# A two-layer hybrid trunk on one core: four quads instead of three begin with the first token half, and partial results move between PSUM banks

## The chip, the core and the metric

One core of a Trainium2 chip runs the whole program. TensorE (PE) multiplies into PSUM, eight banks of 128 x 512 float32 here; VectorE (DVE) and ScalarE (ACT) read PSUM and SBUF; GpSimd (POOL) and SyncE (SP) issue transfers, and POOL computes a few small things. Each of these engines has a queue of its own and works through it in order. The metric is device microseconds for one execution; three were timed before.

## The reference

512 tokens of 1024 features go through two layers: an mLSTM mixer with its MLP, then a short gated convolution with its MLP. All is float32.

```python
def sqrelu_mlp(x, w_up, w_down):
    h = jax.nn.relu(x @ w_up)
    return (h * h) @ w_down

def reference(...):
    for i in range(DEPTH):
        g = norm_g[i]
        h = rms_norm(x, g[0])
        if i % N_MIXERS == 0:
            h = mlstm_mixer(h, ...)
        else:
            h = short_conv_mixer(h, ...)
        x = x + rms_norm(h, g[1])
        h = sqrelu_mlp(rms_norm(x, g[2]), w_mlp_up[i], w_mlp_down[i])
        x = x + rms_norm(h, g[3])
    return x
```

The convolution mixer multiplies x by a 1024 x 3072 matrix, takes three gates from the result, runs a causal three-tap filter over tokens, and multiplies by a 1024 x 1024 matrix.

## The kernel before, in words

Float32 products run as three passes: every operand is split into a high part (ACT casts it to fp32r, line 80) and the remainder (DVE subtracts, line 81), and `mm3` (lines 115 to 117) multiplies high by high, high by low and low by high into the same bank.

The up-projections of the two MLPs and the input product of the convolution (the phases here called mlp 0, conv and mlp 1) are cut into quads. A quad is 512 columns of the weight. It cuts tokens, inner dimension and columns in two and needs seven products of quarter size in place of eight, in the manner of Strassen and Winograd; `prod` is one of the seven, 24 matmuls of 128 x 256. `Seven` makes the token-side factors: `a11` and `a12` from the first token half, and `p1`, `n2`, `r3`, `p4`, `a22` with differences that need the second half. `Quad` makes the weight-side ones: block(0,0) is a, block(0,1) b, block(1,1) d, block(1,0) c; a+b, then a+d, b+d and a+c are summed by DVE in place, and each is split.

Within a quad, x collects f1·a11 (`begin`) and f2·a12 (`first_done`), and is the quarter (0, 0) of the result. y starts as minus the value of x after its first product and takes n2 and r3; z takes p1 and p4; o starts as minus y and takes a22. s5 and s2 are copies of z and y in the middle (lines 875 and 877).

Before a phase stands `last_product` of the phase before. It makes 512 x 1024 in four token tiles of 128, each in two halves of the columns. After each tile comes its tail: mean square (ACT, line 181), the power -0.5 (POOL, line 173), the residual (DVE, line 274), the next norm (line 181, line 173, and DVE at line 252), and eight transposes on PE (line 261). The transposes are put off by `LATE` microseconds of counted matmul time. While the last tile's tail is under way, PE has the work that `enter` gives it: those products of the first `AHEAD` = 3 quads that need the first token half alone. Their bank x comes from the group `pu` (four banks); after the first product minus x is put aside into SBUF (line 843), and `run` copies it back into y (line 858). `last_product` and the down-projection use the group `pd` (two banks), transposes the group `pt` (two).

A scheduler then sets the order within each engine, so the order on the chip is not quite that of the code.

Of the kernel before, what the change touches and what calls it, by code (L numbers as in the profile page):

```python
# [32 lines left out]
LATE = 10.4  # L33
BLOCK = 5.2
PROD = 2.86
AHEAD = 3


@with_exitstack
def tile_hybrid_trunk(  # L40
# [158 lines left out]
    class Seven:  # L199
# [11 lines left out]
        def take(self, t, q, tp):  # L211
            c = slice((t % 2) * P, (t % 2 + 1) * P)
            a = tp.rearrange("p (k n) -> p k n", k=4)
            if t < 2:
                if t == 0:
                    self.keep[q] = raw_tile([4, 256])
                self.part(("a11", "a12")[q], c, a)
                nc.scalar.copy(self.keep[q][:, :, c], a)
                return
            if q == 0:  # L220
                self.first = a
                return
            tt = nc.vector.tensor_tensor
            k0, k1 = (k[:, :, c] for k in self.keep)

            def temp():
                return half_kb().rearrange("p (k n) -> p k n", k=4)

            s22, r3, p1 = temp(), temp(), temp()
            nc.scalar.copy(s22, a)  # L230
            tt(out=p1, in0=self.first, in1=s22, op=ALU.subtract)
            tt(out=r3, in0=self.first, in1=k0, op=ALU.subtract)
            self.part("p1", c, p1)
            tt(out=k0, in0=k0, in1=p1, op=ALU.subtract)
            self.part("n2", c, k0)
            self.part("r3", c, r3)
            tt(out=k1, in0=k1, in1=k0, op=ALU.subtract)
            self.part("p4", c, k1)
            self.part("a22", c, s22)

    def halves(n=2):
        return [slice(i * D // n, (i + 1) * D // n) for i in range(n)]
# [37 lines left out]
    def last_product(wm, r0, hT, g, tail, accs=None, ends=False, ahead=None):  # L280

        flush()
        ws = {}
        parts = [halves() for _ in range(NT)]
        if ends:
            parts[NT - 1] = halves()[:1] + halves(4)[2:]
        ygs = [[] for _ in range(NT)]
        mss = [None] * NT

        def ks(o, t, cs, k0, k1):  # L290
            hf, c0 = divmod(cs.start, 512)
            n = cs.stop - cs.start
            for k in range(k0, k1):
                w = ws[hf][k // 2]
                mm3(
                    o[:, 0:n],
                    rows_of(hT, k, t),
                    (w[:, 0, k % 2, c0 : c0 + n], w[:, 1, k % 2, c0 : c0 + n]),
                    k == 0,
                    k == KO - 1,  # L300
                )

        def done(o, t, cs):
            n = cs.stop - cs.start
            step(BLOCK * n / 512)
            i = len(ygs[t])
            if i == 0:
                mss[t] = small(len(parts[t]))
            yg = half_kb(n=n)
            ygs[t].append((cs, yg))  # L310
            last = i == len(parts[t]) - 1
            o = o[:, 0:n]
            if accs is None:
                part_ms(o, mss[t], i)
                nc.vector.tensor_tensor(out=yg, in0=o, in1=g[:, cs], op=ALU.mult)  # L315
            else:
                y = accs[t][:, cs]
                nc.vector.tensor_tensor(out=y, in0=y, in1=o, op=ALU.add)  # L318
                part_ms(y, mss[t], i)
                eng = nc.vector if ends and t == NT - 1 else nc.gpsimd  # L320
                eng.tensor_tensor(out=yg, in0=y, in1=g[:, cs], op=ALU.mult)
            if last:
                tail(t, ygs[t], mss[t])

        for hf in range(2):
            ws[hf] = [
                piece(
                    wm[r0 + 2 * i * P : r0 + 2 * (i + 1) * P, halves()[hf]].rearrange(
                        "(k p) m -> p k m", p=P
                    ),  # L330
                    2,
                )
                for i in range(4)
            ]
            os = [pd() for _ in range(2)]
            first = KO - 2 if hf == 0 else 0
            for t in range(2):
                ks(os[t], t, parts[t][hf], 0, first)
            for t in range(2):
                ks(os[t], t, parts[t][hf], first, KO)  # L340
                done(os[t], t, parts[t][hf])
        for t in range(2, NT):
            if ahead is not None:
                ahead()
            for cs in parts[t]:
                o = pd()
                ks(o, t, cs, 0, KO)
                done(o, t, cs)
# [457 lines left out]
    class Quad:  # L806
# [27 lines left out]
        def prepare_more(self):  # L834
            self.f2 = self.factor(self.block(1, 0))

        def begin(self):
            self.x = pu()
            prod(self.x, self.f1, self.xT.f["a11"], True)

        def set_aside(self):
            self.s1 = self.values()
            nc.scalar.mul(self.s1, by_tile(self.x), -1.0)

        def first_done(self):
            prod(self.x, self.f2, self.xT.f["a12"], False)
            self.take(0, 0, self.values(), by_tile(self.x))

        def run(self, begun):


            tt = nc.vector.tensor_tensor
            f = self.xT.f
            self.claim()
            a, b = self.block(0, 0), self.block(0, 1)
            y = pu()
            if begun:
                nc.scalar.copy(by_tile(y), self.s1)
            else:
                self.f1 = self.factor(a)  # L860
                self.begin()
                nc.scalar.mul(by_tile(y), by_tile(self.x), -1.0)
            tt(out=a, in0=a, in1=b, op=ALU.add)
            f5 = self.factor(a)
            z = pu()
            if not begun:
                prod(z, f5, f["p1"], True)
            d = self.block(1, 1)
            tt(out=a, in0=a, in1=d, op=ALU.add)
            f6 = self.factor(a)  # L870
            prod(y, f6, f["n2"], False)
            if begun:
                prod(z, f5, f["p1"], True)
            s5 = self.values()
            nc.scalar.copy(s5, by_tile(z))  # L875
            s2 = self.values()
            nc.scalar.copy(s2, by_tile(y))
            c = self.block(1, 0)
            if not begun:
                self.f2 = self.factor(c)  # L880
                self.first_done()
            tt(out=b, in0=b, in1=d, op=ALU.add)
            prod(y, self.factor(b), f["r3"], False)
            o = pu()
            nc.scalar.mul(by_tile(o), by_tile(y), -1.0)
            prod(z, self.factor(d), f["p4"], False)
            tt(out=s5, in0=by_tile(y), in1=s5, op=ALU.add)
            self.take(1, 1, s5, None)
            tt(out=s2, in0=by_tile(z), in1=s2, op=ALU.add)
            self.take(1, 0, s2, None)  # L890
            tt(out=a, in0=a, in1=c, op=ALU.add)
            prod(o, self.factor(a), f["a22"], False)
            self.take(0, 1, self.values(), by_tile(o))

    def enter(quads):


        for qd in quads:
            qd.prepare()
        yield  # L900
        for qd in quads:
            qd.prepare_more()
        yield
        flush(2)
        for qd in quads:
            qd.begin()
            qd.set_aside()
        for qd in quads:
            qd.first_done()
        flush()  # L910

    def by_tile(o):
# [65 lines left out]
    def conv(xT, gain_of, tail_of, ahead):  # L978
# [5 lines left out]
        def gated(p):  # L984
# [10 lines left out]
                nc.gpsimd.memset(u[:, 0, 0:1], 0.0)  # L995

            def take(nh, half, v, o):
                if (nh, half) == (0, 0):
                    nc.scalar.copy(v, o)
                    o = None  # L1000
                got[nh, half] = v if o is None else o
                if (0, half) in got and (1, half) in got:
                    tt(out=uh[:, half], in0=got[0, half], in1=got[1, half], op=ALU.mult)
                if len(got) < 4:
                    return
                for i in range(2):
                    j = 2 * p + i
                    y = ys[0][:, j % 4, :]
                    nc.scalar.mul(y, u[:, i, :], vcol[:, 16 + j : 17 + j])
                    for k in (1, 0):  # L1010
                        n = 2 - k
                        nc.vector.scalar_tensor_tensor(
                            out=y[:, n:],
                            in0=u[:, i, : S - n],
                            scalar=vcol[:, 8 * k + j : 8 * k + j + 1],
                            in1=y[:, n:],
                            op0=ALU.mult,
                            op1=ALU.add,
                        )
# [66 lines left out]
```

## Time and profile before

| | us |
|---|---|
| median of three runs | 1108.69 (1108.65 to 1110.88) |
| the profiled execution | 1110.16 |
| its span, first to last instruction | 1108.4 |
| PE busy | 1081.9 |
| DVE busy | 763.6 |
| ACT busy | 509.4 |
| POOL busy | 72.4 |

The last tail before mlp 0 stands at about 233 to 249 us from the start of the span, that before conv at 580 to 597, and that before mlp 1 at 756 to 772. A row of the timeline gives start, duration, engine, line, operation, what is written and read, and in square brackets how long the engine had been idle and what ended that. A row of the table by windows gives the busy time of each engine in that stretch and, after POOL, the granted PE clock as a share of full speed.

### The profile page before, as it was taken

The numbers are of one execution on the slowest core, as the hardware profiler recorded it, in microseconds if no ns is written. First come the engines' busy times: TensorE is split into PE (matmuls) and PEld (weight loads), VectorE is DVE, ScalarE is ACT, GpSimd is POOL, SyncE is SP. The second block draws the span as 40 slices with busy tenths as digits, with TensorE's granted clock in tenths as the row PEclk, the third lists the DMA queues.
The fourth block names the chain that finished last, engine by engine and source line by source line (L and its number), as shares of the span: only waits on it lengthen the run. The fifth ranks groups of instructions, "written<-read, shape, count | busy, mean of one in ns | idle before, by whom it ended". The sixth has DMA issues, their size and how long they took to land. (4 is left out here: it accounts for less than half of the span.)

```text
span 1108.4 us, 16036 instructions
## 1 busy us (share of the span) xinstructions
PE 1081.9 (98%) x6531; PEld 953.5 (86%) x6531; DVE 763.6 (69%) x1005; ACT 509.4 (46%) x791; POOL 72.4 (7%) x114
## 2 busy tenths in 40 slices
PE   8999999999999999999998999999999999999997
PEld 5878887789899899898888999988989989989986
DVE  5561567489675775757678999948967667675843
ACT  6431545366544343344456555645654424424521
POOL 1100010120000000000131000011000000000011
PEclk9999999999999999999999999999999999999999
DMA  8420264143443143262424363722443413416201
GB/s 266 134 76 1 76 228 143 67 133 115 153 152 114 58 134 103 69 209 82 147 105 135 104 209 115 230 93 95 143 150 127 134 56 116 132 44 205 95 20 57
DMA packets 104783, 133.73 MB, mean 121 GB/s; under 512 B 5221, under 2 KB 76165, under 8 KB 104710
## 3 DMA queue, kind: packets, MB, share of 16 engines
q1 hardware_dynamic: 100246, 116.46, 33.1%
q0 software_dynamic: 4464, 16.25, 4.0%
q8 instruction: 51, 0.84, 0.3%
q14 instruction: 22, 0.18, 0.1%
HBM read 124.31 MB, written 8.39 MB: 120 GB/s over the span
## 5 line engine op out<-in xcount | busy, mean ns | idle before, releaser
L115 PE MATMUL pu<-u 128*128 128x256 f32 (+1 forms) x1424 | 427.5, 300 | 4.2 <-ACT t L875 3.5
L116 PE MATMUL pu<-u 128*128 128x256 f32 (+1 forms) x1424 | 423.8, 298 | 0.5 <-DVE u L81 0.5
L117 PE MATMUL pu<-u 128*128 128x256 f32 (+1 forms) x1424 | 422.8, 298 | 0.0
L81 DVE TENSOR_TENSOR u<-raw,u 128x1024 fp32r<-128x1024 f32 (+1 forms) x270 | 320.2, 1197 | 117.5 <-ACT u L80 116.9
L80 ACT CAST u<-raw 128x1024 fp32r<-128x1024 f32 (+1 forms) x270 | 273.4, 1029 | 210.9 <-PE pd L117 149.6
L115 PEld LDWEIGHTS pu<-u 128*128 128x128 f32 x1424 | 270.5, 190 | 15.9 <-ACT t L875 4.9
L116 PEld LDWEIGHTS pu<-u 128*128 128x128 f32 x1424 | 270.4, 190 | 10.1 <-DVE u L81 1.4
L117 PEld LDWEIGHTS pu<-u 128*128 128x128 f32 x1424 | 269.7, 190 | 8.9 <-DVE u L81 0.3
L115 PE MATMUL pd<-u,hb 128*128 128x512 f32 (+1 forms) x648 | 254.9, 393 | 0.3 <-DVE t L315 0.2
L116 PE MATMUL pd<-u,hb 128*128 128x512 f32 (+1 forms) x648 | 254.1, 392 | 0.0
L117 PE MATMUL pd<-u,hb 128*128 128x512 f32 (+1 forms) x648 | 254.1, 392 | 0.0
L115 PEld LDWEIGHTS pd<-u,hb 128*128 128x128 f32 x648 | 121.8, 188 | 28.7 <-DVE t L315 1.2
L117 PEld LDWEIGHTS pd<-u,hb 128*128 128x128 f32 x648 | 121.7, 188 | 28.2
L116 PEld LDWEIGHTS pd<-u,hb 128*128 128x128 f32 x648 | 121.8, 188 | 27.6 <-DVE u L81 0.6
L963 DVE TENSOR_TENSOR u<-u,pd 128x512 f32<-128x512 f32 x80 | 54.7, 684 | 37.2 <-PE pd L117 37.2
L181 ACT ACTIVATE junk<-u 128x512 bf16<-128x512 f32 (+1 forms) x49 | 30.6, 624 | 73.6 <-DVE u L318 52.8
L80 ACT CAST hb<-t 128x512 fp32r<-128x512 f32 x80 | 48.9, 619 | 25.2 <-DVE t L927 15.5
L81 DVE TENSOR_TENSOR hb<-t,hb 128x512 fp32r<-128x512 f32 x80 | 54.0, 686 | 4.1 <-ACT hb L80 4.1
L924 ACT ACTIVATE t<-pu 128x512 f32<-128x512 f32 x32 | 19.2, 599 | 42.4 <-PE pu L117 42.3
L776 POOL DMA_DIRECT2D u<-xd x12 | 6.4, 535 | 482.2 <-PE pu L117 480.6
L173 POOL TENSOR_TENSOR small<-small,mhalf 128x1 f32<-128x1 f32 x32 | 22.8, 712 | 171.7 <-DVE small L168 161.7
L927 DVE SCALAR_TENSOR_TENSOR t<-pu,t 128x512 f32<-128x512 f32 x32 | 22.0, 688 | 17.2 <-ACT t L924 16.9
(148 smaller groups left out, 682.2 us busy)
## 6 DMA issues: line engine op xcount, KB each, us to landing
raw<-in_w_mlp_up_dram SPq DMA_DIRECT2D x76, 512.0 KB, 4.8
raw<-in_w_mlp_down_dram SPq DMA_DIRECT2D x64, 512.0 KB, 4.5
raw<-in_w_in_conv_dram SPq DMA_DIRECT2D x30, 512.0 KB, 4.7
raw<-in_w_in_mlstm_dram SPq DMA_DIRECT2D x24, 512.0 KB, 4.8
xd<-u POOLq DMA_DIRECT2D x12, 512.0 KB, 3.0
u<-xd POOLq DMA_DIRECT2D x12, 512.0 KB, 6.1
raw<-in_w_out_mlstm_dram SPq DMA_DIRECT2D x8, 512.0 KB, 4.0
raw<-in_w_out_conv_dram SPq DMA_DIRECT2D x8, 512.0 KB, 5.2
```

What stands on the lines that cost most here:

```text
L80: hi = nc.scalar.copy(dst_hi, src)
L81: lo = nc.vector.tensor_tensor(out=dst_lo, in0=src, in1=dst_hi.bitcast(F32), op=ALU.subtract)
L115: nc.tensor.matmul(o, lh, rh, start=first, stop=False, skip_group_check=True)
L116: nc.tensor.matmul(o, lh, rl, start=False, stop=False, skip_group_check=True)
L117: nc.tensor.matmul(o, ll, rh, start=False, stop=last, skip_group_check=True)
L173: nc.gpsimd.tensor_tensor(out=r, in0=r, in1=mhalf[:, 0:1], op=ALU.pow)
L181: nc.scalar.activation(junk(n), src, AF.Square, scale=float(D) ** -0.5, accum_out=ms[:, i : i + 1])
L776: nc.gpsimd.dma_start(xs[t], xd[t])
L924: nc.scalar.activation(c, o, AF.Relu)
L927: nc.vector.scalar_tensor_tensor(out=c, in0=o, scalar=0.0, in1=c, op0=ALU.max, op1=ALU.mult)
L963: nc.vector.tensor_tensor(out=yh, in0=yh, in1=o, op=ALU.add)
```

## The change

`AHEAD` becomes 4. `enter` prepares the fourth quad's two factors in its second stage, and then works in two pairs: both quads begin, then both take their second product. x now comes from `pd`, and minus x goes straight from its bank into y, which has a bank of `pu` from then on until `run`. After the second product x is only copied to SBUF (`put_by`, line 847); the relu or gate of that quarter follows at the end of `run`. z and o of a begun quad come from `pd` too. In `Seven`, `a22` is made first and straight from PSUM. In the phases that add to an accumulator, the product with the gain is written over the accumulator (`yg`) and needs no tile of its own.

```diff
-AHEAD = 3
+AHEAD = 4
...
-            s22, r3, p1 = temp(), temp(), temp()
-            nc.scalar.copy(s22, a)
-            tt(out=p1, in0=self.first, in1=s22, op=ALU.subtract)
+            p1, r3 = temp(), temp()
+            self.part("a22", c, a)
+            nc.scalar.copy(p1, a)
+            tt(out=p1, in0=self.first, in1=p1, op=ALU.subtract)
...
-            self.part("a22", c, s22)
...
-            yg = half_kb(n=n)
+            yg = half_kb(n=n) if accs is None else accs[t][:, cs]
...
-        def begin(self):
-            self.x = pu()
+        def begin(self, bank):
+            self.x, self.y = bank(), pu()
             prod(self.x, self.f1, self.xT.f["a11"], True)
-
-        def set_aside(self):
-            self.s1 = self.values()
-            nc.scalar.mul(self.s1, by_tile(self.x), -1.0)
-
-        def first_done(self):
+            nc.scalar.mul(by_tile(self.y), by_tile(self.x), -1.0)
+
+        def second(self):
             prod(self.x, self.f2, self.xT.f["a12"], False)
-            self.take(0, 0, self.values(), by_tile(self.x))
+
+        def put_by(self):
+            self.v = self.values()
+            nc.scalar.copy(self.v, by_tile(self.x))
...
+            bank = pd if begun else pu
...
-            y = pu()
-            if begun:
-                nc.scalar.copy(by_tile(y), self.s1)
-            else:
+            if not begun:
                 self.f1 = self.factor(a)
-                self.begin()
-                nc.scalar.mul(by_tile(y), by_tile(self.x), -1.0)
+                self.begin(pu)
+            y = self.y
...
-            z = pu()
+            z = bank()
...
-                self.first_done()
+                self.second()
+                self.take(0, 0, self.values(), by_tile(self.x))
...
-            o = pu()
+            o = bank()
...
+            if begun:
+                self.take(0, 0, self.v, None)
...
-        for qd in quads:
+        for qd in quads[:3]:
             qd.prepare()
         yield
-        for qd in quads:
+        for qd in quads[:3]:
+            qd.prepare_more()
+        for qd in quads[3:]:
+            qd.prepare()
             qd.prepare_more()
         yield
         flush(2)
-        for qd in quads:
-            qd.begin()
-            qd.set_aside()
-        for qd in quads:
-            qd.first_done()
+        for two in (quads[:2], quads[2:]):
+            for qd in two:
+                qd.begin(pd)
+            for qd in two:
+                qd.second()
+                qd.put_by()
         flush()
...
-                if (nh, half) == (0, 0):
+                if (nh, half) == (0, 0) and o is not None:
```

On ACT, on the way into mlp 0, the rows around the last tile's transposes were these. The bank pu_2137 is y of the first quad, pu_1957 is x of the second, t2_2033 belongs to the last tile.

```order
L80 CAST u_2140<-raw_2133 128x1024
L843 ACTIVATE t2_1955<-pu_1930 128x512
L843 ACTIVATE t2_1982<-pu_1957 128x512
L843 ACTIVATE t2_2009<-pu_1984 128x512
L858 COPY pu_2137<-t2_1955 128x512
L80 CAST u_2147<-raw_2133 128x1024
L230 COPY t2_2033<-pt_2028 128x512
L80 CAST u_2205<-raw_2135 128x1024
```

At the same place the changed kernel has the following. u_2194 is the split of the first quad's a+d, pd_1966 is x of the second quad, pd_2072 x of the third.

```order
L847 COPY t2_2017<-pd_1939 128x512
L80 CAST u_1897<-pt_2036 128x4x128
L80 CAST u_2194<-raw_2182 128x1024
L231 COPY t2_2041<-pt_2036 128x512
L80 CAST u_2252<-raw_2184 128x1024
L80 CAST u_2281<-raw_2191 128x1024
L80 CAST u_1903<-t2_2041 128x4x128
L80 CAST u_1910<-t2_2042 128x4x128
L847 COPY t2_2070<-pd_1966 128x512
L840 ACTIVATE pu_2073<-pd_2072 128x512
```

The copy that empties the second quad's x (pd_1966) now stands in this queue behind three casts of weights and two of the last tile's parts. Before, each x kept its bank until the relu that takes it, and no bank had to be emptied for the next product.

Somewhat ahead of this, where the last tile's first half is normed, the changed ACT queue has these rows; pd_1939 is x of the first quad and pu_1940 its y, u_1451 holds the tile's residual, and pt_1890 is the third tile's.

```order
L181 ACTIVATE junk_1857,small_1855<-pd_1830 128x512
L181 ACTIVATE junk_1918,small_1855<-pd_1860 128x512
L80 CAST u_1897<-pt_1890 128x4x128
L231 COPY t2_1895<-pt_1890 128x512
L181 ACTIVATE junk_1927,small_1926<-u_1451 128x512
L840 ACTIVATE pu_1940<-pd_1939 128x512
```

Minus x of the first quad stands behind a mean square that needs the last tile's residual.

On PE, at the second quad of mlp 0, the last matmul of p1 (bank pu_2313, z) was followed by 22 of n2 (bank pu_2307, y), and p4 came only after them.

```order
L115 MATMUL pu_2313<-u_1891,u_2310 128x256
L116 MATMUL pu_2313<-u_1891,u_2310 128x256
L117 MATMUL pu_2313<-u_1891,u_2310 128x256
L117 MATMUL pu_2307<-u_1895,u_2317 128x256
L115 MATMUL pu_2307<-u_1895,u_2317 128x256
```

Now p4 (operand u_1914) follows p1 (u_1903) in the same bank, pd_2362, with nothing between, and r3 (bank pu_1967) comes after.

```order
L117 MATMUL pd_2362<-u_1903,u_2359 128x256
L115 MATMUL pd_2362<-u_1914,u_2453 128x256
L116 MATMUL pd_2362<-u_1914,u_2453 128x256
L117 MATMUL pd_2362<-u_1914,u_2453 128x256
L115 MATMUL pd_2362<-u_1914,u_2453 128x256
L116 MATMUL pd_2362<-u_1914,u_2453 128x256
L115 MATMUL pu_1967<-u_1910,u_2424 128x256
```

This pattern, p4 right behind p1, stood in 5 begun quads before and stands in 10 now (three in mlp 0, four in conv, three in mlp 1). In three further places, one in each `enter`, an x takes its second product right behind its first.

## The prediction

> **What bounds the kernel now.** I read the page first, then PE's waits, then the windows around the three tails.
>
> ```profile
> span 1108.4 us, 16036 instructions
> ## 1 busy us (share of the span) xinstructions
> PE 1081.9 (98%) x6531; PEld 953.5 (86%) x6531; DVE 763.6 (69%) x1005; ACT 509.4 (46%) x791; POOL 72.4 (7%) x114
> ```
>
> PE is busy for all but 26.5 us of the span. The change adds no matmul and takes none away, so it can only move PE's idle time and PE's speed. What idles PE:
>
> ```profile
> PE pt L261 <- DVE t L252: 10.1, 6, 3.7
> PE pu L115 <- ACT t L875: 3.5, 5, 0.7
> ```
>
> The first row is the transposes waiting for the last tile's norm, the second a second product that waits for its bank to be copied (0.70 us each, five times). The windows show what the first wait costs besides itself.
>
> ```profile
> 243.08:246.49 3.41, 1.25 (x11) 1.28 (x12) 2.96 (x4) 1.49 (x4) 1.66 (x2) 1.00 0.01 2
> 246.49:249.91 3.42, 3.42 (x18) 3.42 (x17) 2.22 (x3) 2.26 (x3) 0.14 (x1) 0.50 0.47 157
> ...
> 587.83:591.24 3.41, 2.02 (x18) 1.82 (x16) 3.41 (x7) 2.02 (x5) 0.71 (x2) 1.00 0.01 4
> 591.24:594.65 3.41, 1.09 (x9) 0.94 (x10) 2.95 (x4) 2.36 (x4) 1.67 (x2) 1.00 0.37 154
> 594.65:598.07 3.42, 3.42 (x19) 3.42 (x18) 2.96 (x4) 2.27 (x5) 0.39 (x2) 0.50 0.50 156
> ...
> 765.32:768.73 3.41, 1.04 (x10) 0.87 (x9) 2.88 (x6) 2.07 (x5) 1.57 (x1) 1.00 0.01 4
> 768.73:772.15 3.42, 3.42 (x18) 3.42 (x17) 2.20 (x2) 1.21 (x2) 0.00 (x0) 0.50 0.00 0
> ```
>
> After each of three windows of 3.41 us with PE idle for 2.2 to 2.4 us the granted clock is 0.50 for the whole next window: 1.7 us of matmuls lost. The window with 1.39 us idle (3.41 minus 2.02) was followed by full clock. So one idle stretch of 2 us or more is charged nearly twice, and the limit lies between 1.4 and 2.2 us.
>
> The chain behind the wait, before mlp 0:
>
> ```profile
> 242.66 1.23 DVE L81 TENSOR_TENSOR u<-raw,u 128x1024 fp32r<-128x1024 f32 x1
> 242.67 1.63 POOL L173 TENSOR_TENSOR small<-small,mhalf 128x1 f32<-128x1 f32 x1 [2.33 <-DVE small L168]
> 243.97 0.60 ACT L858 COPY pu<-t 128x512 f32<-128x512 f32 x1
> 244.34 1.42 DVE L252 SCALAR_TENSOR_TENSOR t<-u,small,gain 128x512 f32<-128x512 f32 x2 [0.45 <-POOL small L173]
> 245.21 0.42 PEld L261 LDWEIGHTS pt<-ident,t 128*128 128x128 f32 x4 [2.76 <-ACT pu L858]
> 245.24 0.63 PE L261 MATMUL pt<-ident,t 128*128 128x128 f32 x4 [2.60 <-DVE t L252]
> ```
>
> PE stopped at 242.64, after 72 matmuls from 234.08 on (row below): 0.117 us each, 2.8 a product. The norm's two halves ended at 245.76. The same wait before mlp 1:
>
> ```profile
> 234.08 0.37 PE L115 MATMUL pu<-u 128*128 128x256 f32 x1
> ```
>
> ```profile
> 768.05 0.63 PE L261 MATMUL pt<-ident,t 128*128 128x128 f32 x4 [2.37 <-DVE t L252]
> ```
>
> With 1.7 us of lost clock each, the three entries cost 4.3 (mlp 0), 3.7 + 1.7 = 5.4 (conv) and 4.1 us (mlp 1): 13.8 in all. That is what the change could win.
>
> **The entries, worked out.** ACT and DVE take their rows in order, so I walked the changed order with these prices:
>
> ```profile
> 235.09 0.75 DVE L274 SCALAR_TENSOR_TENSOR u<-t,small,u 128x512 f32<-128x512 f32 x1 [0.66 <-POOL small L173]
> 235.76 0.69 DVE L231 TENSOR_TENSOR t<-pt,t 128x512 f32<-128x512 f32 x1
> 236.36 0.68 DVE L232 TENSOR_TENSOR t<-pt,raw 128x512 f32<-128x512 f32 x1
> ```
>
> ```profile
> L81 DVE TENSOR_TENSOR u<-raw,u 128x1024 fp32r<-128x1024 f32 x258 | 312.2, 1221 | 117.1 <-ACT u L80 116.7
> ```
>
> ```profile
> L80 ACT CAST u<-raw 128x1024 fp32r<-128x1024 f32 x258 | 266.2, 1048 | 206.0 <-PE pd L117 149.6 <-DVE raw L863 13.3 <-DVE raw L869 12.9
> ```
>
> ```profile
> L875 ACT COPY t<-pu 128x512 f32<-128x512 f32 x22 | 12.9, 587 | 28.7 <-PE pu L117 28.7
> L885 ACT ACTIVATE pu<-pu 128x512 f32<-128x512 f32 x22 | 12.8, 582 | 14.7 <-PE pu L117 14.7
> ```
>
> A DVE row of 512 takes a slot of 0.60 us (235.76 to 236.36), one of 1024 1.14 (1.22 less the same overlap of 0.08). On ACT they are about 0.5 and 0.95. Bank to bank costs 0.58 against 0.59 into SBUF: the direct move itself is neither gain nor loss, and it saves the copy back (0.60 us at 243.97) on an engine that is no bound.
>
> Mlp 0. (1) The fourth quad's extra split and the sums a+b and b+d now stand in DVE's queue ahead of the last tile's residual, and b+d is on DVE while POOL takes the power. Beside a DVE row of 1024 the power took 1.63 us (242.67); beside nothing DVE waited 0.66 for it (235.09). The residual's first half therefore starts at about 236.7 in place of 235.09. The first quad's minus x stands on ACT behind the mean square of that half: it ends at 238.9, while PE ended the first product at 237.05 and next wants to add to the same bank. **First wait 1.9 us.** (2) 60 matmuls later, at 246.0, PE comes to the transposes. The norm, with its power undisturbed this time, ends at 246.2, so at most 0.3 is lost there: here the longer cover does its work. (3) Then PE takes 4 transposes, 12 matmuls and the third quad's first product, and at 251.1 wants the bank of the second quad's x. DVE from 246.2: split 1.14, relu 0.6, a+d 1.22, to 249.1. ACT then casts a+d (to 250.2), copies p1, casts b+d and d (to 252.6), casts two parts and empties the bank at 254.1. **Second wait 3.0 us.** Behind that copy on ACT stands minus x of the third quad, and PE's fourth begin waits for the copy. Three products later, at 262.6, `enter` is done; unhindered (eight products and 0.9 of transposes from 234.08) it would be 257.4. So 5.2 us are lost, plus 1.7 if the clock falls, against 4.3 before, clock included.
>
> A wait of 3.0 us leaves 2 us in one window of 3.41 unless a window's border falls near its middle; with the wait itself uncertain by 0.7 I give the fall 6 in 10, so 1.0 us. Mlp 0: 6.2 - 4.3 = **+1.9**. Mlp 1 has the same rows in the same order: 6.2 - 4.1 = **+2.1**.
>
> Conv. 90 matmuls stand ahead of the first transposes instead of 72. Minus x of the second quad stands behind the tile's last cast (wait 1.3), the transposes then still wait 0.7, or 1.9 if this collision falls on the sum a+b:
>
> ```profile
> 576.03 1.31 POOL L321 TENSOR_TENSOR t<-u,gain 128x512 f32<-128x512 f32 x1
> 576.04 2.51 DVE L252 SCALAR_TENSOR_TENSOR t<-u,small,gain 128x512 f32<-128x512 f32 x2
> ```
>
> Two such DVE rows took 1.42 at 244.34, so POOL's product held them for 1.1. Written over its input, that product must now wait until the mean square has read it, which moves it some 0.7 later, onto a+b. In this phase the third quad takes its second product right behind its first and waits 1.6 for minus x, which stands behind two casts. Sum 3.6 to 4.8, no single wait of 2 us, so no fall of the clock: I take 4.2, 4.2 - 5.4 = **-1.2**.
>
> **Second product behind first.** Five such waits become ten in `run`: the change names z from the two `pd` banks and the order puts p4 straight behind p1. The price is that of PE's wait on line 875 above: 3.5 us for five, 0.70 each, and some 0.1 until the bank is filled again, 0.8. In the first quad of each MLP nine matmuls of the next quad, 1.05 us, part p1 from p4; ACT may be a little late there, and I charge 0.25 for each. Five more and 0.5: **+4.5**. Nothing hides them, because PE is the bound there and the wait is for ACT on the bank just written; bounds 3 and 6.
>
> **The end.**
>
> ```profile
> 1102.07 0.42 DVE L321 TENSOR_TENSOR t<-u,gain 128x256 f32<-128x256 f32 x1
> 1102.13 0.42 ACT L181 ACTIVATE junk<-u 128x256 bf16<-128x256 f32 x1 [2.33 <-DVE u L318]
> 1102.45 0.19 ACT L181 ACTIVATION_READ_ACCUMULATOR junk<-u 128x1 f32 x1
> 1102.67 0.16 DVE L172 TENSOR_TENSOR small<-small 128x1 f32<-128x1 f32 x1 [0.18 <-ACT junk L181]
> ```
>
> The product with the gain ran beside the mean square. Over its own input it must follow it, and L172 is queued behind it: **+0.4**.
>
> Costed at nothing: six more loads of 512 KB (in the first window above the DMA share is 0.01), hidden behind the third tile's matmuls; if the load of d came late, b+d would and with it everything in (1). The a22 split is only moved.
>
> Sum: 1.9 + 2.1 - 1.2 + 4.5 + 0.4 = +7.7. The profiled execution took 1110.16, 1.76 more than its span; it is 1.5 above the median 1108.69, which I take as the base, since the terms are differences within one trace: **1116.4 us**.
>
> **Rivals.**
> - *The clock does not fall.* If neither 3.0 us wait fills a window, 2.0 goes: 1114.4. Against it: waits of 2.37 and 2.60 brought a fall. Chance 0.18. The Trainium skill, page "TensorE: Matmul & The Clock Gate", Part 1, puts the fall after a whole idle window, about 3.4 us, and advises against idle gaps longer than that. By that rule neither new wait would slow PE; this trace disagrees, with falls after 2.37 and 2.60 us.
> - *The cover works as drawn* (the other side). If DVE and ACT are some 3 us ahead of my walk when the second x is to be emptied, that is if the copy ends by 251.1, the second waits go and no clock falls. The entries then cost about 1 us each, 3 against 13.8; with +4.9 for the rest that is -5.9: 1102.8. For it: 72 matmuls were 2.6 short of the norm, and there are 12 to 18 more. Against: the copy stands behind casts that start only after the norm, in every phase the same. Chance 0.13.
> - *Half of it.* Second waits of 1.5 us and no fall: mlp 0 and mlp 1 3.7 each, conv 3.6, 11.0 - 13.8 + 4.9 = +2.1: 1110.8. Chance 0.13, with what lies around no change.
>
> **How the numbers follow.** My forecast, at least one fall of the clock, has 0.56. A difference of 0.2%, 2.2 us, is about what a measurement of this kernel can tell from none. Faster 0.14, same 0.12, slower 0.74. The range takes in the rival without the fall, the half case and the upper bounds (both clocks fall +1.4, the short waits +1.5, conv +0.6), and leaves out the working cover: 1107.5 to 1120.5.
>
> **What would show it.** Right: PE's waits on line 840 and line 847 in the two MLP entries (about 1.9 and 3.0 us), hardly any on line 252 there, granted clock 0.50 behind the second wait, about ten waits on line 873 of 0.7 us. Wrong: no wait on line 847, or the waits on line 873 staying at five. A DVE queue that is empty when the norm is due would break steps (1) and (3) together.

## The result and the profile after

The changed kernel took 1122.18 us (median of four runs, 1120.55 to 1122.76) against 1108.67 (1108.65 to 1110.88): a ratio of 1.0115, with a 95% interval of 1.0101 to 1.0130. It is slower by 13.5 us, where +7.7 was forecast, and the time lies 1.7 us above the range. The profiled execution took 1122.39.

The head of the page of the changed kernel, and its table of PE's waits (total us, times, longest):

```profile
span 1120.7 us, 16037 instructions
PE 1084.5 (97%) x6531; PEld 954.0 (85%) x6531; DVE 760.7 (68%) x1005; ACT 505.3 (45%) x783; POOL 74.3 (7%) x114
```

```profile
PE pd L115 <- ACT pu L840: 7.0, 4, 2.8
PE pd L115 <- ACT t L873: 6.7, 10, 0.7
PE pd L115 <- ACT t L847: 5.0, 2, 2.6
...
PE pu L115 <- ACT u L80: 1.9, 2, 1.2
```

Of the 10.1 us on L252, 8.7 stood in the three entries; 0.4 us of them is left, as meant (1.9 us on L252 in all). In their place stand 12.0 us for minus x (L840) and for the copy that empties a bank (L847), the ten waits on L873, and a wait of 1.2 us for a weight factor (L80) that the forecast did not have. The windows of 3.41 us at the second wait of mlp 0 and at 680 us, with busy PE, PEld, DVE, ACT, POOL and then the granted PE clock:

```profile
249.88:253.29 3.41, 1.40 (x12) 1.19 (x11) 3.36 (x4) 3.41 (x7) 0.00 (x0) 1.00 0.00 0
253.29:256.70 3.41, 2.85 (x13) 2.85 (x14) 3.41 (x7) 2.23 (x5) 0.00 (x0) 0.50 0.50 153
...
679.96:683.37 3.41, 1.44 (x11) 1.04 (x10) 3.35 (x4) 3.06 (x4) 0.00 (x0) 1.00 0.49 154
683.37:686.78 3.41, 3.41 (x19) 3.41 (x18) 3.41 (x4) 2.25 (x3) 0.00 (x0) 0.50 0.14 31
```

Three falls of the clock again: one in each MLP's entry, as charged, and one at 683 us, where nothing was charged. To place the loss, the start of the same-numbered matmul of the 6531 is compared between two traces. Each column is the time that a stretch took beyond the same stretch of the kernel before (us). Conv I is its entry and about three and a half of its six quads, conv II the rest with its output product and its tails. Each row is one execution, and one fall of the clock more or less moves a column by 1.7. The profiled executions of y first, three everywhere and taps late were 2.9, 2.0 and 1.8 us slower than the medians of these kernels.

```
                      up to mlp 0   mlp 0   conv I   conv II   mlp 1 to end
changed                     +0.27   +3.01    +1.33     +4.21          +3.47
three in conv               -0.19   +1.81    +2.58     +1.73          +1.56
three in the MLPs           +0.24   +1.46    +1.20     +2.62          +1.98
three everywhere            -0.16   +2.37    +2.82     +6.02          +1.15
no taps                     +0.32   +3.27    +0.98     +1.21          +3.22
taps late                   +0.36   +4.48    +1.10     +5.29          +3.43
y first                     +0.52   +0.03    -1.54    +10.89          -1.52
before, y first             +0.43   -1.85    -3.10     +5.92          -0.38
product apart               -0.25   +3.13    -0.52     +4.10          +3.17
copy ahead                  +0.02   -0.27    -0.23     +4.09          +0.34
repairs, three in conv      -0.19   -4.53    -0.81     +3.33          -4.64
repairs, four in conv       +0.33   -4.54    -2.33     +4.21          -4.27
```

The largest single piece of the first row is conv II, where the forecast had nothing. DVE, ACT and PE of the changed kernel there (start, duration):

```profile
672.42 1.22 DVE L861 TENSOR_TENSOR raw<-raw 128x1024 f32<-128x1024 f32 x1
673.55 0.68 DVE L1008 TENSOR_TENSOR raw<-t,t 128x512 f32<-128x512 f32 x1
674.62 0.69 DVE L1008 TENSOR_TENSOR raw<-pd,t 128x512 f32<-128x512 f32 x1 [0.38 <-PE pd L117]
675.22 1.22 DVE L81 TENSOR_TENSOR u<-raw,u 128x1024 fp32r<-128x1024 f32 x1
676.36 2.73 DVE L1017 SCALAR_TENSOR_TENSOR u<-raw,vcol,u 128x511 f32<-128x511 f32 x4
679.00 1.22 DVE L867 TENSOR_TENSOR raw<-raw 128x1024 f32<-128x1024 f32 x1
680.13 1.22 DVE L881 TENSOR_TENSOR raw<-raw 128x1024 f32<-128x1024 f32 x1
681.38 1.23 DVE L81 TENSOR_TENSOR u<-raw,u 128x1024 fp32r<-128x1024 f32 x1
```

```profile
680.31 1.04 ACT L80 CAST u<-raw 128x1024 fp32r<-128x1024 f32 x1 [2.29 <-DVE raw L867]
```

```profile
681.40 0.38 PE L115 MATMUL pu<-u 128*128 128x256 f32 x1 [1.21 <-ACT u L80]
...
682.67 0.39 PE L117 MATMUL pu<-u 128*128 128x256 f32 x1 [0.76 <-DVE u L81]
```

DVE had been waiting itself (0.93 us for PE just before the first of these rows) and works almost without a gap from 672.4 on. ACT has been idle for 2.29 us and waits for the sum a+d (L867), which stands behind the four filter taps (L1017) of the last begun quad. PE, which took a11 and p1 of the next quad meanwhile, needs that factor for n2 at 680.2 and waits 1.21 and then 0.76 us, and here the clock falls for 3.41 us after it: 1.21 + 0.76 + 1.7 = 3.7. In the kernel before, DVE took the same sum (there L869) 7 us ahead of the same taps (L1012):

```profile
665.56 1.23 DVE L869 TENSOR_TENSOR raw<-raw 128x1024 f32<-128x1024 f32 x1
...
672.57 2.73 DVE L1012 SCALAR_TENSOR_TENSOR u<-raw,vcol,u 128x511 f32<-128x511 f32 x4
```

### The profile page after: what moved, and what is told of

The parts are those of the page before. It is cut to its first block, busy times and chain, and to the rows that moved or that the text cites. A ratio compares the mean times of both kernels' runs of the same rounds, so it can differ in the third digit from the quotient of the medians.

```text
span 1120.7 us, 16037 instructions
## 1 busy us (share of the span) xinstructions
PE 1084.5 (97%) x6531; PEld 954.0 (85%) x6531; DVE 760.7 (68%) x1005; ACT 505.3 (45%) x783; POOL 74.3 (7%) x114
## 5 line engine op out<-in xcount | busy, mean ns | idle before, releaser
L80 ACT CAST u<-raw 128x1024 fp32r<-128x1024 f32 (+1 forms) x270 | 272.9, 1028 | 227.0 <-PE pd L117 149.4
L115 PE MATMUL pu<-u 128*128 128x256 f32 (+1 forms) x944 | 290.3, 308 | 1.9 <-ACT u L80 1.9
L116 PE MATMUL pu<-u 128*128 128x256 f32 (+1 forms) x944 | 288.9, 306 | 0.4 <-DVE u L81 0.4
L117 PE MATMUL pu<-u 128*128 128x256 f32 (+1 forms) x944 | 288.1, 305 | 0.8 <-DVE u L81 0.8
L115 PEld LDWEIGHTS pu<-u 128*128 128x128 f32 x944 | 179.2, 190 | 11.7 <-ACT u L80 2.5
L116 PEld LDWEIGHTS pu<-u 128*128 128x128 f32 x944 | 178.9, 190 | 10.0 <-DVE u L81 1.3
L117 PEld LDWEIGHTS pu<-u 128*128 128x128 f32 x944 | 179.0, 190 | 9.6 <-DVE u L81 1.3
L115 PE MATMUL pd<-u 128*128 128x256 f32 x480 | 137.9, 288 | 19.1 <-ACT pu L840 7.0
L116 PE MATMUL pd<-u 128*128 128x256 f32 x480 | 135.7, 283 | 0.0
L117 PE MATMUL pd<-u 128*128 128x256 f32 x480 | 135.6, 283 | 0.0
L115 PEld LDWEIGHTS pd<-u 128*128 128x128 f32 x480 | 91.7, 191 | 22.7 <-ACT t L873 8.8
L116 PEld LDWEIGHTS pd<-u 128*128 128x128 f32 x480 | 91.8, 191 | 0.0
L117 PEld LDWEIGHTS pd<-u 128*128 128x128 f32 x480 | 91.6, 191 | 0.0
```

The source lines that it names most:

```text
L80: hi = nc.scalar.copy(dst_hi, src)
L115: nc.tensor.matmul(o, lh, rh, start=first, stop=False, skip_group_check=True)
L116: nc.tensor.matmul(o, lh, rl, start=False, stop=False, skip_group_check=True)
L117: nc.tensor.matmul(o, ll, rh, start=False, stop=last, skip_group_check=True)
```

## The experiments

All runs below were timed beside the kernel before on the same chip. Its medians were 1109.68 us beside the first four, 1109.49 beside y first (both), product apart and copy ahead, and 1108.85 beside taps late and the two with repairs together.

**Three in conv.** The fourth of the begun quads in conv is its first output gate.

```diff
-        first = quads[:AHEAD]
+        first = quads[:3]
```

> The convolution layer begins three quads again, the two MLPs four. Theory (a begun quad has five products of TensorE work left but nearly all of its VectorE work, so four in a row leave VectorE behind): the waits of 1.21 and 0.76 us at 680 to 683 us and the clock fall behind them (1.7 us) go, with one of the ten 0.7 us waits on L873 (0.84 with its refill) and the 0.5 us at 656: about -5, so 1117 us (1115.5 to 1118.5). Rival (the loss belongs to the weights that arrive there, or to the place of the filter's taps, and not to the number begun): a wait of the same 1 to 2 us stays where the fourth quad runs, time 1121 to 1122.

It took 1118.71 us (1116.23 to 1121.94), ratio 1.0086 (1.0070 to 1.0102). That is just above the theory's range. The waits at 680 went, and conv II fell from +4.21 to +1.73, but conv I rose by 1.25. PE's waits in this kernel at the entry and at the output product:

```profile
603.71 0.39 PE L115 MATMUL pd<-u 128*128 128x256 f32 x1 [2.44 <-ACT t L847]
...
726.64 0.51 PE L115 MATMUL pd<-u,hb 128*128 128x512 f32 x1 [1.57 <-DVE t L315]
```

With three, the third quad still asks for a bank that the copy L847 has to empty, 2.44 us; and part of the gain is given back at 725 us, where the output product waits for a bank that DVE has not read. Of the 4.8 us by which the profiled span is shorter than the changed kernel's, only 1.2 lie in conv; 3.1 lie in the MLPs, which the edit leaves alone and where the clock did not fall in this execution. The edit takes the pair of waits at 680 away, but it is not worth 5 us. In this kernel DVE takes the sum a+d (674.82) ahead of the taps (675.95), as before the change; so the run does not tell the number begun from the order on DVE.

**Three in the MLPs.** The same in the other two phases.

```diff
-        yield from enter(quads[:AHEAD])
+        yield from enter(quads[:3])
...
-            quads[g + 2].run(g + 2 < AHEAD)
+            quads[g + 2].run(g + 2 < 3)
```

> The two MLPs begin three quads, the convolution layer four. Theory (the wait of 2.4 to 2.6 us on L847 at each MLP's entry comes from where the copy stands on ScalarE, behind casts, and not from the number begun): both waits and their clock falls stay, one 0.84 us wait on L873 goes in each MLP: -1.7, so 1120.5 us (1119 to 1122). Rival (the fourth quad's own work makes the entries late): both waits on L847 and both clock falls go with it, -1.7 -2*(2.5+1.7) = -10, so 1112 us.

It took 1118.49 us (1117.92 to 1120.34), ratio 1.0083 (1.0071 to 1.0095), below the theory's range and far from the rival. The ten waits on L873 stayed ten. In mlp 0 the two waits became 1.85 (L840) and 1.88 (L847) in place of 1.42 and 2.58, and only one of the two clock falls in the MLPs was left in this execution. In mlp 1 they were 1.84 and 1.27. So the larger part of the wait on L847 does not belong to the fourth quad. In conv II, which the edit leaves alone, the pair of waits at 680 was there (1.13 and 0.76) without a fall of the clock: +2.62 in place of +4.21. How much of the 3.7 us in the medians is the clock alone, this run does not tell.

**Three everywhere.** Both edits.

> Three quads begin in all three layers, the rest of the change is kept. Theory (the parts add up, -5 and -1.7): 1115.5 us (1114 to 1117), so about half of the loss belongs to the number begun and half to the way in which the first products are finished later. Rival (all of the loss comes from the fourth quad): 1108 to 1110 us, as before the change.

It took 1120.66 us (1118.99 to 1122.70), ratio 1.0102 (1.0087 to 1.0116): a miss. The parts do not add up. Conv II lost 6.0 us, most of it in one wait of 3.07 us on L315 at 729 us and the clock fall beside it. But the rival falls too: with three quads everywhere the change costs nearly as much as with four, so most of its loss does not belong to the fourth quad.

**No taps.** The run leaves out the two shifted taps of the third gated quad's filter, four instructions and 2.73 us of DVE.

```diff
-                    for k in (1, 0):
+                    for k in (1, 0) if p != 2 else ():
```

> Leaves out part of the computation: the two shifted taps of the filter on the gated product of the third quad of the convolution layer (four VectorE instructions, 2.73 us, at 676.36 us). Theory (VectorE is behind): the wait of 1.21 us at 680.2 and that of 0.76 at 681.9 go, and with them the clock fall: -3.7, so 1118.5 us (1117.5 to 1119.5). Rival (the weights of the next quad arrive late): both waits stay, 1121.5 to 1122.5.

It took 1119.12 us (1117.84 to 1119.51), ratio 1.0085 (1.0072 to 1.0098): conv II falls by 3.0, to +1.21. Of the pair of waits at 680 one of 0.41 us is left, and there is no clock fall. The next quad's weights were there in time; DVE was not.

**Taps late.** The four instructions are kept and issued after the next quad's first split of a+d.

```diff
             f6 = self.factor(a)
+            while late:
+                with tc.issue_after(last_lo[0]):
+                    late.pop()()
...
+                if p == 2:
+                    late.append(taps)
+                else:
+                    taps()
```

> The change is kept and nothing is left out; the four VectorE instructions of the third gated quad's filter stand behind the next quad's sum L867 and its factor's L81 instead of ahead of them. Theory of the amount (VectorE has more work than four begun quads leave time for, wherever the taps stand): the waits of 1.21 and 0.76 us at 680 us come back a little later on the casts that now stand behind the taps, and the time stays at 1121 to 1123. Theory of the place (VectorE is late for one product only, by less than the 2.73 us of the taps): both waits and the clock fall go, as when the taps are left out: 1118.5 to 1119.5 us.

It took 1123.06 us (1120.49 to 1124.81), ratio 1.0131 (1.0111 to 1.0150), no gain. PE's waits in this kernel (its line numbers are two higher):

```profile
704.08 0.39 PE L117 MATMUL pu<-u 128*128 128x256 f32 x1 [1.11 <-ACT u L80]
705.34 0.38 PE L119 MATMUL pu<-u 128*128 128x256 f32 x1 [0.76 <-DVE u L81]
731.94 0.50 PE L117 MATMUL pd<-u,hb 128*128 128x512 f32 x1 [1.26 <-DVE t L317]
```

The same pair of waits comes back one quad later, at 704 us, and another at the output product; conv II stands at +5.29 in place of +4.21. (mlp 0 stands 1.5 higher, too, where its clock fell for two windows in this execution.) DVE ahead of the pair:

```profile
699.03 2.73 DVE L1031 SCALAR_TENSOR_TENSOR u<-raw,vcol,u 128x511 f32<-128x511 f32 x4
701.68 1.22 DVE L869 TENSOR_TENSOR raw<-raw 128x1024 f32<-128x1024 f32 x1
```

These are the taps of the fourth gated quad, which the edit does not move, and the sum a+d of the last quad. In the changed kernel the sum came first (694.1 against 700.2), here it stands behind them. So the time is what the theory of the amount expects, to 0.1 us, but the run does not rule out the place: in all 13 traces a wait of more than 1 us for this factor (L80) stands in conv where a sum a+d follows directly on four taps, and nowhere else. Whether the amount of DVE's work or its order is at the root stays open.

**y first.** `run` copies y's bank right after n2, ahead of the copy of z; y's product r3 can then stand between p1 and p4.

```diff
             prod(y, f6, f["n2"], False)
+            s2 = self.values()
+            nc.scalar.copy(s2, by_tile(y))
             if begun:
                 prod(z, f5, f["p1"], True)
             s5 = self.values()
             nc.scalar.copy(s5, by_tile(z))
-            s2 = self.values()
-            nc.scalar.copy(s2, by_tile(y))
```

> The change is kept; in run() the copy of y's second product is written ahead of the copy of z, so that it can run while z's first product does. Theory (TensorE waits on L873 because y's copy stands behind z's on ScalarE and y's third product follows at once): all ten waits of 0.67 us go, 10 * 0.84 = -8.4, so 1114 us (1112.5 to 1116). Rival (the time is kept elsewhere, because the engines behind, VectorE above all, set the pace of a begun quad): the waits go from L873, but others of the same sum come on L80 or L81, and the time stays within 1121 to 1123.

It took 1115.59 us (1113.34 to 1118.49), ratio 1.0045 (1.0031 to 1.0059). All ten waits went. mlp 0 gained 3.0 on the changed kernel, conv I 2.9, mlp 1 5.0 (1.7 of it a fall of the clock that stayed away); conv II lost 6.7 in this execution, the slowest of five, with three windows of half clock. What happened there, in the waits and the timeline of this kernel:

```profile
PE pd L115 <- DVE t L315: 4.6, 2, 4.4
```

```profile
718.15 1.05 ACT L80 CAST u<-raw 128x1024 fp32r<-128x1024 f32 x1 [1.65 <-DMA raw<-in_w_mlp_up_dram]
```

```profile
720.97 6.90 DVE L81 TENSOR_TENSOR u<-raw,u 128x1024 fp32r<-128x1024 f32 x6
727.78 1.28 DVE L315 TENSOR_TENSOR t<-pd,gain 128x512 f32<-128x512 f32 x2
```

Six splits of weights stand in DVE's queue ahead of the two L315 that empty PE's banks, and they start late because casts on ACT had waited for the loads of the next phase's weights; DVE itself had been idle for 3.34 us shortly before. So both expectations hold, each in its phase: in the MLPs the waits were real cost, in conv the time gained is lost at its end.

**y first in the kernel before.** The same exchange there.

> The kernel before the change, with the same exchange of two copies and nothing else. Theory: its five waits of 0.70 us on L875 go, 5 * 0.87 = -4.4, so 1104.3 to 1105.3 us beside 1108.7 to 1109.7 of before: faster than both kernels. Rival (the pace is set behind): no change.

It took 1111.39 us (1107.60 to 1113.60), ratio 1.0011 (0.9999 to 1.0023): no gain. Of the five short waits the three in conv went; one of 0.73 us in each MLP stayed. The table shows the rest: -3.10 in conv I, and +5.92 in conv II, where its waits have the same row. (The -1.85 in mlp 0 is mostly the clock, which did not fall after the wait of 2.59 us there.)

```profile
PE pd L115 <- DVE t L315: 3.4, 2, 3.2
```

**Product apart.** The product with the gain gets its own tile again.

```diff
-            yg = half_kb(n=n) if accs is None else accs[t][:, cs]
+            yg = half_kb(n=n)
```

> The change is kept, but the product on POOL (L309) goes to a tile of its own again instead of being written in place. Theory (in place, POOL's addition L321 stands beside VectorE's L861 at 587.7 us and makes it 2.31 instead of 1.22 us): the first wait of the convolution layer's entry falls from 2.77 to 1.7 us, -1.1, so 1121 us (1120 to 1122). Rival (the place of the result does not matter): no change, 1122.2.

It took 1118.34 us (1117.90 to 1121.16), ratio 1.0078 (1.0064 to 1.0093). The profiled span is 3.0 shorter than the changed kernel's, 1.85 of it in conv I, where the first wait fell from 2.77 to 1.04 us, and 0.3 behind the last matmul. The direction was right and the size too small, because there are two costs. POOL and DVE of the changed kernel before conv:

```profile
573.87 1.29 POOL L321 TENSOR_TENSOR u<-u,gain 128x512 f32<-128x512 f32 x1 [2.93 <-ACT junk L181]
575.12 0.55 POOL L173 TENSOR_TENSOR small<-small,mhalf 128x1 f32<-128x1 f32 x1
```

```profile
575.70 1.42 DVE L274 SCALAR_TENSOR_TENSOR u<-u,small 128x512 f32<-128x512 f32 x2 [1.72 <-POOL small L173]
...
587.75 2.31 DVE L861 TENSOR_TENSOR raw<-raw 128x1024 f32<-128x1024 f32 x1
```

And the same instructions with the tile of its own:

```profile
571.96 1.29 POOL L321 TENSOR_TENSOR t<-u,gain 128x512 f32<-128x512 f32 x1 [3.75 <-DVE u L318]
573.66 0.55 POOL L173 TENSOR_TENSOR small<-small,mhalf 128x1 f32<-128x1 f32 x1 [0.41 <-DVE small L168]
```

```profile
574.24 1.42 DVE L274 SCALAR_TENSOR_TENSOR u<-t,small,u 128x512 f32<-128x512 f32 x2 [0.66 <-POOL small L173]
...
586.33 1.23 DVE L861 TENSOR_TENSOR raw<-raw 128x1024 f32<-128x1024 f32 x1
```

In place, the product waits until ACT's mean square has read its input, and the power L173, queued behind it on POOL, waits with it: the residual L274 waits 1.72 instead of 0.66, and DVE has hardly a gap in which to make that up before conv's entry. And one product lands on the sum L861, which takes 2.31 instead of 1.23.

**Copy ahead.** The second quad's copy L847 is issued ahead of the last tile's casts on ACT. To that end the tile's transposes are held back until the copy is issued.

```diff
-        while queue and queue[0][0] <= 0:
+        while queue and queue[0][0] <= 0 and not held[0]:
...
+                held[0] = qd is quads[1]
...
-                qd.put_by()
+                done = qd.put_by()
+                if held[0]:
+                    held[0] = False
+                    with tc.issue_after(done):
+                        step(0)
```

> The change is kept, but ScalarE's copy L847 of the second quad's first quarter stands ahead of the casts for the next norm tile at each layer's entry. Theory (TensorE's second wait at an MLP's entry is for that copy behind the casts): the two waits of 2.58 and 2.42 us on L847 shrink to under 1 us, and the clock falls behind them go: -2*(1.6 to 2.0) -3.4, so 1115.3 us (1114 to 1117.5). Rival (the casts themselves set when the third quad can begin): the wait turns into one on L80 or on L252's transposes of the same size, and the time stays at 1121 to 1123.

It took 1114.33 us (1114.08 to 1115.45), ratio 1.0040 (1.0027 to 1.0053). ACT in the changed kernel, and after it the same copy in this one (here L849):

```profile
249.80 0.58 ACT L231 COPY t<-pt 128x512 f32<-128x512 f32 x1
250.28 2.00 ACT L80 CAST u<-raw 128x1024 fp32r<-128x1024 f32 x2
252.17 1.14 ACT L80 CAST u<-t 128x512 fp32r<-128x512 f32 x2
253.21 0.58 ACT L847 COPY t<-pd 128x512 f32<-128x512 f32 x1
```

```profile
247.34 0.59 ACT L849 COPY t<-pd 128x512 f32<-128x512 f32 x1 [2.14 <-PE pd L117]
```

5.9 us earlier, and the copy's waits are gone from PE's table. mlp 0 stands at -0.27 and mlp 1 at +0.34 against the kernel before, although each has four of the short waits (L875 here) where the kernel before had one. No wait on the casts or transposes that now come later shows in the MLPs, so the rival falls.

**Repairs together.** Copy ahead, product apart, and y first in the MLPs only; once with three begun quads in conv, once with four and the late taps. The code is that of the single runs, and quads take an argument that says whether y is copied first.

```diff
-            return Quad(w_up[i], g * 512, g * 512 + 256, xT, take)
+            return Quad(w_up[i], g * 512, g * 512 + 256, xT, take, y_first=True)
```

> The change with four repairs: the copy L847 of the second quad ahead of the casts, the product L309 in a tile of its own, in the MLPs the copy of y's product ahead of that of z's, and three begun quads in the convolution layer. If the parts add up: 1114.3 (with the copy moved) - 2.5 (the tile) - 5 (the copies in the MLPs) - 2 to -4 (the convolution layer), so 1104 to 1106 us, faster than before (1109.5). If speed in the convolution layer is given back at its end (the wait of 1.7 to 4.6 us on L315 at 725 us that three runs with a faster layer showed): 1106.5 to 1109.

> As the run with four repairs, but four begun quads in the convolution layer, and the taps of the third gated quad behind the next quad's factor. If the place of the taps was the cause: 1114.3 - 2.5 - 5 - 3.5 = 1103.5, within 1 us of the run with three; if the amount of VectorE's work is: 1107 to 1108.

With three in conv it took 1103.56 us (1101.13 to 1104.66), ratio 0.9954 (0.9938 to 0.9969); with four 1104.26 (1102.40 to 1105.74), ratio 0.9962 (0.9948 to 0.9976). Both beat the kernel before and the changed one, and the first lies 0.4 us below the sum expected of the parts. The profile of the first (its L843 is L840, its L879 L873):

```profile
span 1101.3 us, 16029 instructions
PE 1076.3 (98%) x6531; PEld 948.8 (86%) x6531; DVE 762.8 (69%) x1005; ACT 503.7 (46%) x782; POOL 71.5 (6%) x114
```

```profile
PE pd L115 <- ACT pu L843: 5.8, 5, 1.7
...
PE pd L115 <- ACT t L879: 2.1, 3, 0.7
```

No wait of 2 us or more is left in the entries and the clock does not fall from the entry of mlp 0 until 1098 us; PE is busy 5.6 us less than before for the same matmuls. The MLPs stand about 4.5 us below the kernel before, each; conv II still stands 3.3 above. There the pair of waits is back, with three begun quads, and again DVE has the taps ahead of the sum:

```profile
671.27 0.38 PE L115 MATMUL pu<-u 128*128 128x256 f32 x1 [1.23 <-ACT u L80]
...
672.53 0.38 PE L117 MATMUL pu<-u 128*128 128x256 f32 x1 [0.76 <-DVE u L81]
```

With four, the time is the one expected of the theory of the place (1103.5) and not of the amount (1107 to 1108), yet the pair is not gone: it stands at 691 us (1.09 and 0.76), as in the run with late taps, and conv II at +4.21, with -2.33 in conv I. The two come out alike, but they differ in the place of the taps as well, so they do not show by themselves what the number begun is worth.

## Why the prediction was wrong, point by point

- **The direction and the mechanism in the MLPs: right.** Waits on L840 and L847 of 1.42 and 2.58 us (forecast 1.9 and 3.0) and a clock fall. mlp 0's entry is 1.42 + 2.58 + 1.7 - 4.3 = +1.4 for a forecast +1.9, mlp 1's 1.43 + 2.42 + 1.7 - 4.1 = +1.45 for +2.1. The waits were shorter than forecast (4.0 us for 5.2) and the falls, charged at 0.6 each, came both, so the two misses cancel in part. Moving the copy removed the second wait, as step (3) has it.
- **Second product behind first: right.** Ten gaps of 0.84 less five of 0.87: +4.0 for +4.5. In the MLPs the exchange of copies gave all of it back.
- **The entry of conv: the sum right, by luck in part.** 2.77 + 0.39 + 1.39 - 5.4 = -0.85 for -1.2. But the first wait was twice the 1.3 of the forecast, and the forecast had no single wait of 2 us there and so no fall of the clock. A wait of 2.77 us came, and the clock stayed at 1.00 because the border of a window split it, 1.40 us idle in one and 1.37 in the next; in five other runs (three in the MLPs, no taps, y first, copy ahead, taps late) the same wait of 2.8 to 2.9 us was followed by a fall. The collision of POOL's product with the sum a+b, which the forecast named as possible, came. The delay of the power behind that product was missed; it was seen for the end of the kernel only, though the same code runs in all tails that add to an accumulator.
- **The failing step: conv's sum stops at its entry.** The forecast counted waits on ACT and nothing for DVE between the quads of conv. Over the span DVE is busy for 69%, but from 620 to 680 us of the kernel before it was busy for 57.6 of 60 us. The change also turned an order on DVE: the next quad's sum a+d went from 7 us ahead of four taps to right behind them, its factor came late, and PE waited: 1.21 + 0.76 + 1.7 = +3.7, with 0.5 more at 656 us. Leaving the taps out took 3.0 of it away. That PE's waits come from this order is what the traces show; that four begun quads in a row leave DVE with too much work is the likely reason behind it, and was only argued. The 1.7 for the clock is a matter of the window again: without the fall, conv II cost +2.62.
- **The end: right.** The product stands behind the mean square as charged: from the last L318 to the last residual 2.28 us pass, where it was 1.95, +0.33 for +0.4. The spans do not show it, since behind that residual the profiled execution of before took 0.37 us more.
- **The sum of these points.** Without the end the terms come to 7.3 - 0.5 - 0.65 - 0.5 + 0.35 + 4.2 = 10.2, where the last matmul starts 12.3 later.
- **The rest.** Of the 2.1 that no term holds, 0.9 lie in conv I, 0.5 in conv II, 0.4 in mlp 1 and 0.3 ahead of mlp 0, and their cause stays open. The spans, too, differ by 12.3, and the medians by 13.5, since the profiled execution of before lay 1.5 above its median and that of the changed kernel 0.2. Among 11 runs of before the quickest, 1106.95, had a mean granted clock of 0.996 and the slowest, 1110.70, 0.994: the number of clock falls is the likely cause of that scatter, which was only argued.
- **The rivals.** *The cover works as drawn* needed the copy to end by 251.1; with the copy ahead it ended at 247.9, and then the change comes out ahead of the old entries (mlp 0 at -0.27 with 2.5 of new short waits in it), so that rival's mechanism was sound and its condition not met. *The clock does not fall* did come in one run: with three in conv, the same 2.58 us wait left the clock at 1.00.

## What to carry to other kernels

When work is put ahead of a wait, look at what its results occupy: here the extra products needed a bank that one copy had to empty, and that copy stood behind five casts in its engine's queue; one issue order was worth about 8 us. When a group of work loses a part of PE's share, read the load of the other engines in that stage and not over the span (57.6 of 60 us against 69%), and compare the order of every queue before and after, also where no wait stands today: here one sum had slipped behind four instructions on DVE. And a gain in one phase has to be followed to the phase's end, where queued weight splits gave it back.

## What the runs showed of the hardware

Whether a wait of 2.4 to 2.8 us halves the clock depends on where the border of a window falls in it. Windows follow one another every 3.41 us (the falls of the changed kernel start at 253.29, 683.37 and 785.77, which is 126 and 30 windows apart), with a phase of their own in each execution. In the kernel with three in conv (windows counted back from its one fall, at 604.08 us), a wait as long as that of the changed kernel is split:

```profile
253.39 0.39 PE L115 MATMUL pd<-u 128*128 128x256 f32 x1 [2.58 <-ACT t L847]
```

```profile
249.12:252.53 3.41, 1.69 (x15) 1.49 (x13) 3.06 (x4) 3.41 (x6) 0.00 (x0) 1.00 0.00 1
252.53:255.95 3.42, 2.56 (x22) 2.56 (x22) 3.42 (x6) 2.39 (x5) 0.00 (x0) 1.00 0.45 140
```

1.72 us idle in one window, and no fall; in the changed kernel 2.01 and 1.97 us (3.41 less 1.40 and 1.44) were followed by 0.50. Counted from the falls of each of the 13 traces, at full clock no window with less than 1.6 us idle was followed by a fall and every one with 1.9 or more was; in between both came. The Trainium skill, page "TensorE: Matmul & The Clock Gate", Part 1, says that the window is free-running, and the different phases agree; it puts the fall after at least one idle window of about 3.4 us, and these windows with PE busy for 1.4 of 3.41 us disagree.

A POOL product can hold a DVE instruction up for most of its own length: the sum L861 of 1.23 us took 2.31, 1.08 more, where a product of 1.29 us started on POOL at nearly the same time (587.69 against 587.75).
